# Layer-1 modulation summed along rows on VectorE, the first feature tile started by itself, and the row norm applied by a diagonal matmul

## The chip, the cores and the metric

The kernel runs on 1 core of a Trainium2 chip. Its engines are named as in the profile: PE (TensorE matmul; PEld is its weight load), DVE (VectorE), ACT (ScalarE), POOL (GpSimd) and SP (SyncE, which issues most of the DMAs). The metric is device time in microseconds (us) of one execution; lower is better. All times inside an execution count from the start of the profiled span.

## The reference

Two decoder layers on x of 512 tokens by 2048 features, in float32. Only the head of layer 1 matters here:

```python
c_act = jax.nn.silu(c)                               # c: (1, 2048)
mod = (c_act @ ada_w[0] + ada_b[0])[:, None, :]      # ada_w[0]: (2048, 6144)
shift, scale, gate = jnp.split(mod, 3, axis=-1)
h = rmsnorm(x, norm_g[0]) * (1.0 + scale) + shift    # x * rsqrt(mean(x*x) + eps) * g, then modulated
proj = h @ w_in                                      # w_in: (2048, 12288), then retention, gate, w_out
x = x + gate * y
```

The features of `h` are the contraction of `h @ w_in`, so a product with feature tile kt (128 features) can be made as soon as shift and scale of those 128 features are known. Each of the 2048 values of shift and of scale is a sum over 2048 inputs.

## The kernel before

Every product that matters is made in three float32r passes (high times high, high times low, low times high). Each operand is therefore split: ACT makes the high part with a copy to float32r (`split`, L132), DVE subtracts it from the original for the low part (L133).

**First stage (L434 to L574).** The 2048 features are 16 feature tiles, taken as 8 units of two. For each unit the stage accumulates the first head's products with three column blocks of `w_in`: "qk" (4 PSUM banks), "g" (3 banks) and "v" (4 banks), 11 outputs of 128x512, two feature tiles, three passes: 66 matmuls per unit (`products`, L403, issued at L413). PSUM has 8 banks, four in the group `acc` and four in `aux`. "g" holds three `aux` banks throughout and one is left for transposes; "qk" and "v" take turns in the four `acc` banks. When they change places, `swap` (L391) has ACT copy each bank's partial sums out to SBUF (L397) and the other's back in (L401), eight copies per change.

**Order.** `queued` (L429) pins each piece of work behind what stands last on ACT, DVE, PE and SP, so on these engines the program order is the order written. Each engine works through its own list in that order and waits at an instruction whose inputs are late.

**Modulation.** For each unit 16 tiles `aw` (`load_shift_scale`, L363) hold 2048 input rows by 256 shift and 256 scale columns, inputs on partitions (one partition has 16 of the inputs). `add_row` (L371) weights them with silu(c) and adds them up: the first on ACT (L374), the rest as 15 DVE operations of 128x512 (L376). Then PE sums over partitions with a column of ones (`sum_columns`, L385), 8 products of one column. `make_first` (L501) adds bias and norm gain (`modulate`, L245 to L249) and ACT makes h of both feature tiles twice, rounded (L268) and full (L270); DVE subtracts for the low part (L271). The rows of a unit are added up during the unit before it; the last DVE sums, PE's column sums and `make_first` stand just ahead of the products that use them.

**x and the vectors.** x arrives as eight tiles with tokens on partitions. Each token's factor rsqrt(mean square) comes from squares on ACT and DVE (`square`, L448) and a power on POOL (L128). `normalise` (L458) multiplies x by it, half on ACT (L459), half on DVE (L460). Then PE transposes each feature tile (`transpose`, L482) and ACT copies it to `xT` (L487); four tiles go ahead of the first products, two more in each unit. Ten small vectors come in by ten DMAs on POOL's queue (L229) and are turned by PE into `vcol`.

**After the stage.** DVE works out the rotary tables (`tables`, L278 to L302) after its last work on unit 7, ACT takes their sine and cosine (L304, L305), and ACT's first weight cast of the next stage (the last "g" bank of head 0, `g_r`) is queued behind them. That stage's products stand at L158 to L160.

Of the kernel before, what the change touches and what calls it, by code (L numbers as in the profile page):

```python
# [16 lines left out]
P = 128  # L17
# [32 lines left out]
def hybrid_trunk_kernel(  # L50
# [19 lines left out]
    decay,  # L70
    x_t,
    out,
):
# [27 lines left out]
    def tmp(name, shape=(P, T)):  # L101
        return base.tile(list(shape), F32, tag="tmp", bufs=6, name=name)
# [111 lines left out]

    vrows = tmp("vrows", (P, 2, P))
    DVE.memset(vrows[:, 1, :], 0.0)
    for r0, n, which, src in (
        (0, 32, 0, ada_b[0, 0 : 2 * D]),
        (32, 32, 0, ada_b[1, 0 : 2 * D]),
        (64, 16, 0, norm_g[0]),  # L220
        (80, 16, 0, norm_g[1]),
        (96, 32, 0, ret_gn_g[0]),
        (0, 4, 1, mla_q_norm_g[0]),
        (4, 4, 1, mla_kv_norm_g[0]),
        (8, 16, 1, ada_b[0, 2 * D :]),
        (24, 16, 1, ada_b[1, 2 * D :]),
        (40, 16, 1, final_norm_g),
    ):
        POOL.dma_start(vrows[r0 : r0 + n, which, :], src.rearrange("(r p) -> r p", p=P))  # L229
    vcol = base.tile([P, P + 56], F32, name="vcol")  # L230
    bias_c = (vcol[:, 0:32], vcol[:, 32:64])
    norm_c = (vcol[:, 64:80], vcol[:, 80:96])
# [9 lines left out]
    def modulate(i, ps_shift, ps_scale, k0, n):  # L242
# [3 lines left out]
        if ps_scale is not None:  # L246
# [5 lines left out]
            )  # L252

    def columns(ps, name):

        mc = small(name, 4)
        junk = tmp(f"{name}_d")
        for b in range(4):
            DVE.scalar_tensor_tensor(
                out=junk[:, b * P : (b + 1) * P], in0=ps[:, b * P : (b + 1) * P], scalar=1.0, in1=ident,  # L260
                op0=ALU.mult, op1=ALU.mult, accum_out=mc[:, b : b + 1],
            )
        return mc

# [82 lines left out]
    def first_load(kind, u):  # L347

        cn = 384 if kind == "g" else 512
        tags = (("k4b", 4), ("k4b", 4)) if kind == "g" else (("whi", 3), ("wlo", 3))  # L350
        raw = base.tile([P, 2, cn], F32, tag="raw", bufs=3, name=f"{kind}0_{u}_raw")
        c0 = {"v": 4096, "g": 8192}.get(kind)
        for dst, src in qk_parts(0, u) if kind == "qk" else [(whole, rows(w_ret_in, u, 2, c0, cn))]:
            nc.sync.dma_start(dst(raw), src)

        def prepare():
            hl = [base.tile([P, 2, cn], F32R, tag=t, bufs=n, name=f"{kind}0_{u}_{t}{i}") for i, (t, n) in enumerate(tags)]
            split(raw, *hl)
            loaded[kind, u] = hl

        return prepare

    def load_shift_scale(u, i):  # L363

        aw = l0p.tile([P, 2, 2, 256], F32, tag="aw", bufs=9, name=f"aw_{u}_{i}")
        for s in range(2):
            c0 = s * D + u * 256
            nc.sync.dma_start(aw[:, :, s, :], ada0[:, 2 * i : 2 * i + 2, c0 : c0 + 256])
        return aw

    def add_row(am, aw, k, first):  # L371
        ck = cact[:, k : k + 1]
        if first:
            ACT.activation(am, aw[:, k % 2], AF.Identity, scale=ck)  # L374
        else:
            DVE.scalar_tensor_tensor(out=am, in0=aw[:, k % 2], scalar=ck, in1=am, op0=ALU.mult, op1=ALU.add)  # L376

    def sum_columns(u, am, rest=()):

        ps = aux(f"mc_{u}")  # L380
        terms = [(aw[:, k % 2], cact[:, k : k + 1]) for k, aw in rest] + [(am, crow)]
        nt = len(terms)
        for i, (src, col) in enumerate(terms):
            for c_ in range(4):
                PE.matmul(  # L385
                    ps[:, c_ * nt + i : c_ * nt + i + 1], src[:, c_ // 2, c_ % 2 * P : (c_ % 2 + 1) * P], col,
                    start=True, stop=True,
                )
        return ps, nt

# [49 lines left out]
    first_aw = []  # L440
    for i in range(NU):
        first_aw.append(queued(load_shift_scale, 0, i))
    prepares = {("qk", 0): queued(first_load, "qk", 0)}

# [12 lines left out]

    def normalise(t):  # L458
        ACT.activation(xs[t][0], xs[t][0], AF.Identity, scale=norm[t])  # L459
# [5 lines left out]
    am = l0p.tile([P, 2, 256], F32, tag="am", bufs=2, name="am_0")  # L465
    queued(square, 0)
    queued(square, 1)
    queued(normalise, 0)
    queued(square, 2)
    queued(normalise, 1)  # L470
    queued(square, 3)
    queued(normalise, 2)
    for k in range(2):
        queued(add_row, am, first_aw[0], k, k == 0)
    queued(normalise, 3)

    xT = [k4(f"xT_{u}", F32) for u in range(NU)]

    def transpose(kt):
        ps = aux(f"xT_ps_{kt}")  # L480
        for t in range(NT):
            PE.transpose(  # L482
                ps[:, t * P : (t + 1) * P],
                xs[t][kt // 8][:, (kt % 8) // 4, (kt % 4) * P : (kt % 4 + 1) * P],
                ident,
            )
        return lambda: ACT.copy(xT[kt // 2][:, kt % 2, :], ps)  # L487

    DIRECT = 14
    for kt in range(4):  # L490
        queued(queued(transpose, kt))
    vps = aux("vps")
    queued(PE.transpose, vps[:, 0:P], vrows[:, 0, :], ident)
    queued(PE.transpose, vps[:, P : 2 * P], vrows[:, 1, :], ident)
    for k in range(2, DIRECT):
        queued(add_row, am, first_aw[k // 2], k, False)
    queued(DVE.tensor_copy, vcol, vps[:, 0 : P + 56])
    queued(prepares["qk", 0])
    mc = queued(sum_columns, 0, am, [(k, first_aw[k // 2]) for k in range(DIRECT, KD)])

    def make_first(u, mc):  # L501
        mc, nt = mc
        if nt > 1:
            sums_ = small(f"mc_{u}", 4)
            DVE.tensor_reduce(
                out=sums_, in_=mc[:, 0 : 4 * nt].rearrange("p (c i) -> p c i", i=nt), axis=AX.X, op=ALU.add
            )
            mc = sums_
        modulate(0, mc[:, 0:2], mc[:, 2:4], 2 * u, 2)
        for kt in (2 * u, 2 * u + 1):  # L510
            hT[kt] = big(f"hT_{kt}")
            yield make_h(0, kt, xT[u][:, kt % 2, :], hT[kt])

    for low in list(queued(lambda: list(make_first(0, mc)))):
        queued(low)
    swap(None, "qk")
    banks["g"] = [aux(f"g0_{b}") for b in range(3)]
    for u in range(NU):

        here, there = ("qk", "v") if u % 2 == 0 else ("v", "qk")  # L520
        more = u + 1 < NU
        aw = []
        if u > 0:
            prepares[here, u] = queued(first_load, here, u)
        prepares["g", u] = queued(first_load, "g", u)
        if more:
            aw += [queued(load_shift_scale, u + 1, i) for i in range(2)]
        prepares[there, u] = queued(first_load, there, u)
        if more:
            aw += [queued(load_shift_scale, u + 1, i) for i in range(2, NU)]  # L530
        if u > 0:
            queued(prepares[here, u])
        queued(prepares["g", u])
        if more:
            am = l0p.tile([P, 2, 256], F32, tag="am", bufs=2, name=f"am_{u + 1}")
            queued(add_row, am, aw[0], 0, True)
        lows = queued(lambda: list(make_first(u, mc))) if u > 0 else ()
        ahead = [2 * u + 4, 2 * u + 5] if 2 * u + 5 < KD else []
        if ahead:
            queued(queued(transpose, ahead[0]))  # L540
        for k in range(1, 4) if more else ():
            queued(add_row, am, aw[k // 2], k, False)
        for low in lows:
            queued(low)
        queued(prepares[there, u])
        if more:
            for k in range(4, KD):
                queued(add_row, am, aw[k // 2], k, False)
# [5 lines left out]
        if ahead:  # L554
            queued(queued(transpose, ahead[1]))
# [14 lines left out]
        queued(products, there, 2 * u)  # L570
        if more:
            mc = queued(sum_columns, u + 1, am)
        queued(products, there, 2 * u + 1)
# [1360 lines left out]
```

## Time and profile before

| | |
|---|---|
| median of 3 runs | 2227.26 us (2224.17 to 2229.06) |
| the profiled execution | 2223.61 us, its span 2221.8 us |
| PE busy, share of the span | 98% |
| DVE busy | 71% |
| ACT busy | 45% |
| first product of the first stage starts | 32.92 us |
| last product of the first stage starts | 172.62 us |
| mean granted clock of PE | 0.996 |

PE is busy nearly throughout, but its busy time is pipelined and modelled, so the stage at hand has to be read from the order of starts, not from the share. What the change touches lies in the first 190 us of the span. In a row of the timeline the first number is the start, the second the length (of a group, from its first start to its last end), and a bracket gives the engine's idle time before it and what ended it.

### The profile page before, as it was taken

Reading aid. Unit: us, or ns where it says so; the run is one execution under the profiler, and the core shown is the slowest. Engines: PE = TensorE matmul, PEld = TensorE weight load, DVE = VectorE, ACT = ScalarE, POOL = GpSimd, SP = SyncE. Lnnn points to the kernel's source line nnn. Section 1 sums busy time; section 2 is a strip of 40 time slices with the busy share of each in tenths; the row PEclk is TensorE's granted clock in tenths of the full one; section 3 lists DMA queues with packets and bytes.
Section 4 is the critical chain, followed back from the end, with each engine's and each line's share of the span. In section 5 each row is a group of like instructions: output and inputs, shape, how many; then the busy total and the mean of one; then the engine's idle time right before and its main releaser. Section 6 shows DMA issues by size and latency. Waiting matters only on the chain.

```text
span 2221.8 us, 28357 instructions
## 1 busy us (share of the span) xinstructions
PE 2170.8 (98%) x10414; PEld 1819.9 (82%) x10414; DVE 1586.6 (71%) x2397; ACT 998.5 (45%) x1496; POOL 104.2 (5%) x184
## 2 busy tenths in 40 slices
PE   5999999999999999999999999999999999999997
PEld 4887888888888888888888888898888888888886
DVE  7888867767676789656676777567977677776545
ACT  5664433434343444434344445345444355554443
POOL 1000000000001000010000000010001000000000
PEclk9999999999999999999999999999999999999998
DMA  9974586766767678573646465453458723225332
GB/s 343 353 241 168 191 282 202 261 224 218 262 198 274 220 263 296 174 239 127 232 153 226 147 211 187 137 172 108 161 185 294 251 77 95 76 96 189 123 125 90
DMA packets 238396, 437.15 MB, mean 197 GB/s; under 512 B 21032, under 2 KB 98992, under 8 KB 238256
## 3 DMA queue, kind: packets, MB, share of 16 engines
q1 hardware_dynamic: 225664, 396.16, 54.2%
q0 software_dynamic: 12160, 38.90, 4.4%
q8 instruction: 81, 1.33, 0.2%
q14 instruction: 59, 0.48, 0.1%
q10 hardware_dynamic: 432, 0.27, 0.0%
HBM read 392.27 MB, written 42.99 MB: 196 GB/s over the span
## 4 chain that ended last, share of the span: by engine, by line
PE 75%; DVE 11%; ACT 5%; issue 5%; DMA 2%; POOL 0%; SPq 0%; DVEq 0%; POOLq 0%; ACTq 0%
PE o L1161 13%; PE qk L160 4%; PE qk L158 4%; PE qk L159 4%; PE o L1861 4%; DVE am L376 2%; PE x L702 2%; PE y L703 2%; PE x L703 2%; PE y L701 2%; PE y L702 2%; PE x L701 2%; PE s L703 2%; PE s L702 2%; PE s L701 2%
## 5 line engine op out<-in xcount | busy, mean ns | idle before, releaser
L1161 PE MATMUL o<-o_h,o_whi 128*128 128x512 f32 (+1 forms) x496 | 192.5, 388 | 0.0
L1161 PE MATMUL o<-o_h,o_wlo 128*128 128x512 f32 (+1 forms) x496 | 191.6, 386 | 0.0
L1161 PE MATMUL o<-o_l,o_whi 128*128 128x512 f32 (+1 forms) x496 | 191.5, 386 | 0.0
L160 PE MATMUL qk<-hT,qk_l 128*128 128x512 f32 x448 | 175.0, 391 | 0.4 <-DVE qk_l L133 0.4
L158 PE MATMUL qk<-hT,qk_h 128*128 128x512 f32 x448 | 174.9, 390 | 0.0
L159 PE MATMUL qk<-hT,qk_h 128*128 128x512 f32 x448 | 174.5, 389 | 0.0
L864 DVE SCALAR_TENSOR_TENSOR mod_am<-mod_aw,cact,mod_am 128x1024 f32<-128x1024 f32 x120 | 153.5, 1280 | 13.5 <-DMA mod_aw<-in_ada_w_dram 12.8
L133 DVE TENSOR_TENSOR o_wlo<-o_r,o_whi 128x1024 fp32r<-128x1024 f32 x61 | 74.5, 1222 | 84.9 <-ACT o_whi L132 84.9
L133 DVE TENSOR_TENSOR qk_l<-qk_r,qk_h 128x1024 fp32r<-128x1024 f32 x56 | 68.1, 1223 | 67.7 <-ACT qk_h L132 67.3
L1161 PEld LDWEIGHTS o<-o_h,o_wlo 128*128 128x128 f32 x496 | 93.2, 188 | 18.7
L1161 PEld LDWEIGHTS o<-o_l,o_whi 128*128 128x128 f32 x496 | 93.3, 188 | 18.3
L1161 PEld LDWEIGHTS o<-o_h,o_whi 128*128 128x128 f32 x496 | 93.3, 188 | 18.1
L160 PEld LDWEIGHTS qk<-hT,qk_l 128*128 128x128 f32 x448 | 84.1, 188 | 19.4 <-DVE qk_l L133 2.1
L159 PEld LDWEIGHTS qk<-hT,qk_h 128*128 128x128 f32 x448 | 84.1, 188 | 17.3
L158 PEld LDWEIGHTS qk<-hT,qk_h 128*128 128x128 f32 x448 | 84.2, 188 | 17.2
L132 ACT CAST qk_h<-qk_r 128x1024 fp32r<-128x1024 f32 x56 | 57.8, 1049 | 88.7 <-PE qk L159 73.5
L376 DVE SCALAR_TENSOR_TENSOR am<-aw,cact,am 128x512 f32<-128x512 f32 x118 | 88.7, 751 | 3.6
L158 PE MATMUL g<-h,g_h 128*128 128x512 f32 x232 | 90.7, 391 | 0.3 <-ACT g_h L132 0.3
L159 PE MATMUL g<-h,g_h 128*128 128x512 f32 x232 | 90.4, 389 | 0.0
L160 PE MATMUL g<-h,g_l 128*128 128x512 f32 x232 | 89.9, 390 | 0.0
L132 ACT CAST o_whi<-o_r 128x1024 fp32r<-128x1024 f32 x61 | 63.5, 1052 | 21.9 <-issue 10.1
L133 DVE TENSOR_TENSOR o_w_lo<-o_w_raw,o_w_hi 128x1024 fp32r<-128x1024 f32 x32 | 38.9, 1220 | 34.6 <-ACT o_w_hi L132 34.5
(1256 smaller groups left out, 5996.0 us busy)
## 6 DMA issues: line engine op xcount, KB each, us to landing
mod_aw<-in_ada_w_dram SPq DMA_DIRECT2D x128, 512.0 KB, 5.3
aw<-in_ada_w_dram SPq DMA_DIRECT2D x128, 256.0 KB, 6.0
o_r<-in_ret_w_out_dram SPq DMA_DIRECT2D x64, 512.0 KB, 4.4
qk_r<-in_ret_w_in_dram SPq DMA_DIRECT2D x112, 256.0 KB, 3.8
g_r<-in_mla_w_in_dram SPq DMA_DIRECT2D x32, 512.0 KB, 4.3
o_w_raw<-in_mla_w_out_dram SPq DMA_DIRECT2D x32, 512.0 KB, 3.8
qk_d<-qk_st POOLq DMA_DIRECT2D x32, 256.0 KB, 3.7
qk_r<-qk_d SPq DMA_DIRECT2D x32, 256.0 KB, 6.3
```

Of the source, the lines that this page charges most:

```text
L132: ACT.copy(hi, src)
L133: DVE.tensor_sub(lo, src, hi.bitcast(F32))
L158: PE.matmul(o, lhs[0], rhs[0], start=first and not seeded, stop=False, skip_group_check=seeded)
L159: PE.matmul(o, lhs[0], rhs[1], start=False, stop=False, skip_group_check=seeded)
L160: return PE.matmul(o, lhs[1], rhs[0], start=False, stop=last, skip_group_check=seeded)
L376: DVE.scalar_tensor_tensor(out=am, in0=aw[:, k % 2], scalar=ck, in1=am, op0=ALU.mult, op1=ALU.add)
L701: PE.matmul(banks[b], a[0], w[0], start=first, stop=False, skip_group_check=True)
L702: PE.matmul(banks[b], a[0], w[1], start=False, stop=False, skip_group_check=True)
L703: PE.matmul(banks[b], a[1], w[0], start=False, stop=True, skip_group_check=True)
L864: DVE.scalar_tensor_tensor(out=am, in0=aw, scalar=ck, in1=am, op0=ALU.mult, op1=ALU.add)
L1161: PE.matmul(o, w[i][:, ki, c0 + b * P : c0 + (b + 1) * P], a[j], start=first and i + j == 0, stop=last and i == 1, skip_group_check=True,)
L1861: PE.matmul(banks2[b][:, cols], w[0][i][:, 0, b * P : (b + 1) * P], o2_moving(w, u, cols)[j], start=u + i + j == 0, stop=u == KD - 1 and i ...
```

## The change

- The weights of shift and scale come from a transposed copy of `ada_w[0]` made with the inputs, outputs on partitions: one tile `aw` of 128 outputs by 2048 inputs for each feature tile and each of shift and scale, four buffers of it instead of nine of the old. One DVE operation multiplies it by silu(c) and sums along the row (`sum_mod`); nothing is left for PE. Feature tile 0 is loaded and summed in two halves.
- For that silu(c) must stand on every partition: c is loaded to one partition, PE spreads it with four float32 products of 128x512 with ones, and ACT takes their silu (`c_all`), ahead of the squares.
- `make_first` works on one feature tile. The stage starts with tile 0 alone, "v" first: v(0), g(0), a swap, qk(0), qk(1), g(1), a swap, v(1).
- In each unit u the preparation of unit u+1 is now written ahead of the products of u (`prepare_ahead`: the casts of all three weight tiles and h of the first feature tile), and the second tile's h behind the swap (`prepare_behind`).
- The token factor is no longer multiplied into x: DVE makes a diagonal of it, and the transposes become matmuls with that diagonal. Six tiles go ahead of the first products.
- The ten small vectors are laid out with the inputs and come by one DMA.

What each engine gets in one unit, in program order (unit u's products, unit k = u+1 prepared; "here" and "there" are "qk" and "v", which change places from unit to unit):

```
SP    here(k), aw(2k,shift), aw(2k,scale), g(k), aw(2k+1,shift), there(k), aw(2k+1,scale)
DVE   sum(2k,shift), low of here(k), sum(2k,scale), a and b of 2k, sum(2k+1,shift), low h(2k),
      low of g(k), sum(2k+1,scale), a and b of 2k+1, low of there(k), low h(2k+1)
ACT   high of here(k), h(2k) twice, high of g(k), high of there(k), xT copy, 8 swap copies, h(2k+1) twice, xT copy
PE    here(2u), here(2u+1), diagonal matmuls, g(2u), g(2u+1), there(2u), diagonal matmuls, there(2u+1)
```

The diff, cut to its core:

```diff
-    def load_shift_scale(u, i):
-        aw = l0p.tile([P, 2, 2, 256], F32, tag="aw", bufs=9, name=f"aw_{u}_{i}")
...
+    def load_mod(kt, s):
+        aw = l0p.tile([P, D], F32, tag="aw", bufs=4, name=f"aw_{kt}_{s}")
+        n = 2 if kt == 0 else 1
+        for j in range(n):
+            cols = slice(j * D // n, (j + 1) * D // n)
+            nc.sync.dma_start(aw[:, cols], ada_t[s * D + kt * P : s * D + (kt + 1) * P, cols])
         return aw
-    def add_row(am, aw, k, first):
-    def sum_columns(u, am, rest=()):
...
+    def sum_mod(kt, s):
+        aw, n = mods[kt, s], 2 if kt == 0 else 1
+        col = small(f"mc_{kt}_{s}", n)
+        for j in range(n):
+            cols = slice(j * D // n, (j + 1) * D // n)
+            DVE.scalar_tensor_tensor(
+                out=aw[:, cols], in0=aw[:, cols], scalar=1.0, in1=c_all[:, cols], op0=ALU.mult, op1=ALU.mult,
+                accum_out=col[:, j : j + 1],
+            )
...
+    c_all = l0p.tile([P, D], F32, name="c_all")
+    ACT.dma_start(c_all[0:1, :], c)
+    for j in range(4):
+        cols = slice(j * T, (j + 1) * T)
+        ps = aux(f"c_ps{j}")
+        PE.matmul(ps, ones[0:1, :], c_all[0:1, cols], start=True, stop=True)
+        ACT.activation(c_all[:, cols], ps, AF.Silu)
...
-    def normalise(t):
-        ACT.activation(xs[t][0], xs[t][0], AF.Identity, scale=norm[t])
-        DVE.tensor_scalar(out=xs[t][1], in0=xs[t][1], scalar1=norm[t], scalar2=None, op0=ALU.mult)
+    def diagonal(t):
+        diags.append(l0p.tile([P, P], F32, tag="diag", bufs=4, name=f"x_diag{t}"))
+        DVE.tensor_scalar(out=diags[t], in0=ident, scalar1=norm[t], scalar2=None, op0=ALU.mult)
...
-            PE.transpose(
+            PE.matmul(
                 ps[:, t * P : (t + 1) * P],
                 xs[t][kt // 8][:, (kt % 8) // 4, (kt % 4) * P : (kt % 4 + 1) * P],
-                ident,
+                diags[t], start=True, stop=True,
             )
...
+    def prepare_ahead(u, first=None):
+        here, there = ("qk", "v") if u % 2 == 0 else ("v", "qk")
+        low = queued(prepares[here, u])
+        queued(sum_mod, 2 * u, 0)
+        if first is not None:
+            queued(first)
+        queued(low)
+        queued(sum_mod, 2 * u, 1)
+        low = queued(make_first, 2 * u)
+        queued(sum_mod, 2 * u + 1, 0)
+        queued(low)
+        low = queued(prepares["g", u])
+        late[u] = queued(prepares[there, u])
+        queued(low)
+        queued(sum_mod, 2 * u + 1, 1)
+
+    def prepare_behind(u):
+        low = queued(make_first, 2 * u + 1)
+        queued(late[u])
+        queued(low)
+
+    load_unit(1)
+    queued(queued(prepares["v", 0]))
+    for s in range(2):
+        queued(sum_mod, 0, s)
+    low = queued(make_first, 0)
+    queued(sum_mod, 1, 0)
+    queued(low)
+    lows = [queued(prepares[kind, 0]) for kind in ("g", "qk")]
+    for low in lows:
+        queued(low)
+    queued(sum_mod, 1, 1)
+    swap(None, "v")
+    queued(products, "v", 0)
...
+    queued(products, "g", 0)
+    queued(swap, "v", "qk")
+    low = queued(make_first, 1)
+    queued(products, "qk", 0)
+    prepare_ahead(1, low)
...
         if more:
             queued(swap, here, there)
+            prepare_behind(u + 1)
```

More of the change, by code (lines that the diff above doesn't have):

```diff
@@ L213, in hybrid_trunk_kernel @@
     ACT.activation(cact, cact, AF.Silu)
[L215 to L229, printed above, removed]
     vcol = base.tile([P, P + 56], F32, name="vcol")
+    POOL.dma_start(vcol, vecs)
     bias_c = (vcol[:, 0:32], vcol[:, 32:64])
@@ L252, in modulate @@
             )
[L254 to L263, printed above, removed]
     def make_h(i, kt, src, dst):
@@ L391, in swap, with make_first @@
+    def make_first(kt):
+        k1 = slice(kt, kt + 1)
+        DVE.tensor_add(b_col[0][:, k1], mods[kt, 0], bias_c[0][:, k1])
+        DVE.scalar_tensor_tensor(
+            out=a_col[0][:, k1], in0=mods[kt, 1], scalar=bias1[:, k1], in1=norm_c[0][:, k1], op0=ALU.add, op1=ALU.mult
+        )
+        hT[kt] = big(f"hT_{kt}")
+        return make_h(0, kt, xT[kt // 2][:, kt % 2, :], hT[kt])
     def swap(old, new):
@@ L494, in hybrid_trunk_kernel @@
[L494 to L512, printed above, removed]
@@ L514, in hybrid_trunk_kernel, with load_unit @@
-    for low in list(queued(lambda: list(make_first(0, mc)))):
-        queued(low)
-    swap(None, "qk")
-    banks["g"] = [aux(f"g0_{b}") for b in range(3)]
-    for u in range(NU):
+    def load_unit(u):
+        here, there = ("qk", "v") if u % 2 == 0 else ("v", "qk")
+        load_first(here, u)
+        load_mods(2 * u)
+        load_first("g", u)
+        mods[2 * u + 1, 0] = queued(load_mod, 2 * u + 1, 0)
+        load_first(there, u)
+        mods[2 * u + 1, 1] = queued(load_mod, 2 * u + 1, 1)
@@ L520, in hybrid_trunk_kernel @@
+    queued(products, "g", 0)
[3 more added lines that the diff above has]
+    prepare_ahead(1, low)
+    queued(products, "qk", 1)
+    queued(queued(transpose, 6))
+    queued(products, "g", 1)
+    queued(swap, "qk", "v")
+    prepare_behind(1)
+    queued(queued(transpose, 7))
+    queued(products, "v", 1)
+    for u in range(1, NU):
         here, there = ("qk", "v") if u % 2 == 0 else ("v", "qk")
         more = u + 1 < NU
-        aw = []
-        if u > 0:
-            prepares[here, u] = queued(first_load, here, u)
@@ L525, in hybrid_trunk_kernel @@
-        prepares["g", u] = queued(first_load, "g", u)
+        ahead = [2 * u + 6, 2 * u + 7] if 2 * u + 7 < KD else []
         if more:
[L527 to L548, printed above, removed]
+            load_unit(u + 1)
@@ L570, in hybrid_trunk_kernel @@
         queued(products, there, 2 * u)
-        if more:
-            mc = queued(sum_columns, u + 1, am)
+        for kt in ahead[1:]:
+            queued(queued(transpose, kt))
         queued(products, there, 2 * u + 1)
```

78 lines of the change are left out of this document (42 added, 36 removed).

## The prediction

> **What bounds the stage now.** I read the windows first (start:end, length, then busy time of PE, PEld, DVE, ACT and POOL, the granted clock, DMA share, GB/s), then the timelines of DVE, PE and ACT for one unit, then those of the start and of the end.
>
> ```profile
> span 2221.8 us, 28357 instructions
> 8.00:14.00 6.00, 0.95 (x2) 0.37 (x2) 4.04 (x10) 5.18 (x7) 2.29 (x4) 1.00 1.03 408
> 48.00:50.00 2.00, 0.76 (x7) 0.49 (x5) 1.97 (x3) 0.45 (x1) 0.00 (x0) 1.00 1.10 347
> 52.00:54.00 2.00, 2.00 (x6) 1.52 (x5) 1.93 (x4) 2.00 (x4) 0.00 (x0) 0.50 1.10 348
> 60.00:100.00 40.00, 39.95 (x193) 32.65 (x192) 36.85 (x53) 27.87 (x44) 0.00 (x0) 1.00 1.09 353
> L376 DVE SCALAR_TENSOR_TENSOR am<-aw,cact,am 128x512 f32<-128x512 f32 x118 | 88.7, 751 | 3.6
> 85.17 1.22 DVE L133 TENSOR_TENSOR v_wlo<-v_raw,v_whi 128x1024 fp32r<-128x1024 f32 x1
> 86.31 0.95 DVE L133 TENSOR_TENSOR g_k4b<-g_raw,g_k4b 128x768 fp32r<-128x768 f32 x1
> ...
> 102.48 1.22 DVE L133 TENSOR_TENSOR qk_wlo<-qk_raw,qk_whi 128x1024 fp32r<-128x1024 f32 x1
> 85.53 0.95 PE L385 MATMUL mc<-ones,am 128*128 128x1 f32 x8
> ...
> 95.10 0.60 PE L482 MATMUL xT_ps<-ident,x 128*128 128x128 f32 x4
> 95.45 4.38 PE L413 MATMUL g<-hT,g_k4b 128*128 128x512 f32 x18
> 99.67 0.39 PE L413 MATMUL qk<-hT,qk_whi 128*128 128x512 f32 x1
> ...
> 100.57 0.39 PE L413 MATMUL qk<-hT,qk_whi 128*128 128x512 f32 x1
> ```
>
> A unit takes 17.3 us (low of "here" to low of "here", 85.17 to 102.48). Of that PE's products need 15.0: 18 of "g" in 4.22 (95.45 to 99.67) and 48 at 0.225 (99.67 to 100.57 is four); two transposes add 0.35 each, so 15.7, which no rearrangement here can beat. The column sums (85.53) take 0.95, which makes 16.7 and leaves 0.6 for all of PE's waits. DVE needs 15 adds x 0.751 = 11.3, two lows of 1.14 (85.17 to 86.31), one of 0.95 and smaller ones: it is busy 92% from 60 to 100, close behind PE. DMA runs at 353 GB/s there. So with the column sums gone and nothing else in PE's way a unit could gain 1.6.
>
> **The start.** Columns: start, length, idle before and its releaser.
>
> ```profile
> 14.63 1.22 DVE L450 SCALAR_TENSOR_TENSOR x_sq<-x 128x1024 f32<-128x1024 f32 x1 [0.26 <-DMA x<-in_x_dram]
> 15.78 0.08 DVE L450 DVE_READ_ACCUMULATOR x_sq<-x 128x1 f32 x1
> 17.41 1.15 ACT L459 ACTIVATE x<-x,x_r 128x1024 f32<-128x1024 f32 x1 [0.50 <-POOL x_r L128]
> 19.13 0.58 ACT L487 COPY xT<-xT_ps 128x512 f32<-128x512 f32 x1 [0.56 <-PE xT_ps L482]
> 19.98 0.58 ACT L487 COPY xT<-xT_ps 128x512 f32<-128x512 f32 x1 [0.27 <-PE xT_ps L482]
> 32.92 0.80 PE L413 MATMUL qk<-hT,qk_whi 128*128 128x512 f32 x1 [0.67 <-ACT hT L268]
> 33.51 0.63 PE L413 MATMUL qk<-hT,qk_wlo 128*128 128x512 f32 x1
> 33.94 0.63 PE L413 MATMUL qk<-hT,qk_whi 128*128 128x512 f32 x1
> 1487.48 0.68 PE L906 MATMUL x_r<-x_diag,ones 128*128 128x128 f32 x4
> ```
>
> Gone ahead of the first product are 14 adds, PE's column sums, the vectors' transposes and 1.15 on ACT plus the DVE half of `normalise`. The last token factor is there at 17.41, its diagonal about 17.65. Ahead of the squares ACT now also waits for PE to spread c: four cold products, 0.43 each at the cold rate of 33.51 to 33.94, and four silus; some of that lies beside the wait for x, so I put the last diagonal at 18.0 (17.65 to 18.4). The page "FP8 and Floating Point Precision" of the Trainium skill (Matmul Precision, TensorE Precision Notes) says that true float32 takes four passes through PE; by that the four would cost 1.72 each. The four float32 products of 128x128 at 1487.48 took 0.68 together, at most 0.17 each, which does not look like four passes; the rule stays as a rival below.
>
> From 18.0 on: six transposed tiles go through ACT 0.85 apart (19.13 to 19.98), and only then comes the high of v(0) (1.05), its low on DVE (1.14), and only behind that the four half sums. A sum over 1024 takes 1.15 and a read of 0.08 (14.63, 15.78): 1.23, with the two adds and `make_first` about 5.65 in all. Sum: 18.0 + 0.5 + 6 x 0.85 + 1.05 + 1.14 + 5.65 puts the first h at 31.1 to 31.4, and with one ACT operation (0.82) the first product at 32.0 instead of 32.92. So the start gains 1 us, not the ten that the removed adds suggest: `aw` is there, but the sums are queued behind v's low and that behind six copies.
>
> **The loop in each unit.** The rows that carry it:
>
> ```profile
> 78.55 0.59 ACT L487 COPY xT<-xT_ps 128x512 f32<-128x512 f32 x1 [3.88 <-PE xT_ps L482]
> 79.04 0.59 ACT L397 COPY part_qk<-qk 128x512 f32<-128x512 f32 x1
> ...
> 83.91 1.05 ACT L132 CAST v_whi<-v_raw 128x1024 fp32r<-128x1024 f32 x1
> 84.86 0.84 ACT L132 CAST g_k4b<-g_raw 128x768 fp32r<-128x768 f32 x1
> 85.60 0.72 ACT L374 ACTIVATE am<-aw,cact 128x512 f32<-128x512 f32 x1
> 87.62 0.82 ACT L268 ACTIVATE hT<-xT,b_col,a_col 128x512 fp32r<-128x512 f32 x1 [1.30 <-DVE a_col L249]
> 88.35 0.80 ACT L270 ACTIVATE h_6f<-xT,b_col,a_col 128x512 f32<-128x512 f32 x1
> 33.60 0.69 DVE L271 TENSOR_TENSOR hT<-h_0f,hT 128x512 fp32r<-128x512 f32 x1 [1.65 <-ACT h_0f L270]
> ```
>
> A sum over 2048 isn't in this trace. From the row of 1024: 1.15, 1.06 for 1024 elements more (DVE's lows go from 0.69 at 512 to 1.22 at 1024, 0.53 per 512) and 0.08 of read, 2.3. Bounds: 2.0 (the adds' 0.751 at 512 against 1.15 at 1024, 0.4 per 512) and 3.0 (four times 0.751); I take 2.30, whose row has the same form with a sum along the row. DVE's work falls from about 17.0 to 9.2 + 2 x 1.14 + 0.9 + 2 x 0.69 + 0.6 = 14.4 per unit, below PE's 15.7. DVE is no longer the bound by its sum; but the program order closes a loop over three engines. With S the first copy of a swap in unit u:
> - swap, eight copies on ACT, 4.87 (79.04 to 83.91); then h of the second tile, 0.73 and 0.80 (87.62, 88.35): S+6.4;
> - DVE's low of that h, 0.65: S+7.05; only behind it the sum of the next unit's first shift, 2.30: S+9.35;
> - the high of the next "here" takes one of three weight buffers, whose last reader is "there" just swapped in: after the eighth copy 3 products, the transposes and 12 products (3.8), S+8.95, and 1.05 on ACT: S+10.0; its low on DVE, 1.14: S+11.2;
> - the sum of scale, 2.30: S+13.5; b and a, 0.15 each as an estimate (the read's 0.08 and a gap): S+13.8;
> - h of the next first tile twice, high of "g", high of "there", one copy to `xT`, in ACT's order and start to start 0.73 + 0.7 + 0.74 + 0.95 + 0.49 (78.55 to 79.04) = 3.6: S+17.4. Only there stands the next swap.
>
> So a unit takes 17.4, with PE waiting some 1.7 of it at the four banks that the swap fills 1.24 apart. The last units without transposes come to 16.9 and 16.5, the first to 16.7: S(0) to S(6) is 16.7 + 3 x 17.4 + 16.9 + 16.5 = 102.3, plus 0.1 for the hand-overs of each of six periods: 102.9. From the first h (31.1) to S(0) goes another chain of DVE and ACT: the four long sums 9.2, the lows of h, "g" and "qk" 2.7, b and a, a second h, and 3.6 on ACT: 17.7, S(0) = 48.8. S(6) = 151.7. From there 4.98 for the swap, 15 products (3.4) and the last unit's 66 (14.95): the last product ends at **175.0**.
>
> New transfers: one row of 8 KB per partition and tile instead of pieces of 1 KB. Bytes per unit stay 5.6 MB, 16.0 us at the 353 GB/s of the window, 13.8 at the 408 of the x loads: either is hidden in 17.4. The ten small loads become one; nothing waits for them. The diagonal products cost 0.35 to 0.68 a tile (rows 95.10 and 1487.48), I take 0.4; PE's slack of 1.7 hides it, and without that slack it would cost 0.1 to 0.7 per unit.
>
> **The end of the stage.**
>
> ```profile
> 161.87 0.43 DVE L282 CAST ret_sin<-ret_pi 128x512 f32<-128x512 int32 x1 [0.38 <-DMA ret_pi<-in_positions_dram]
> 171.94 1.07 PE L413 MATMUL qk<-hT,qk_whi 128*128 128x512 f32 x4
> 172.31 0.63 ACT L304 ACTIVATE ret_sin<-ret_sin 128x512 f32<-128x512 f32 x1 [5.36 <-DVE ret_cos L302]
> 174.53 0.50 PE L158 MATMUL g<-hT,g_h 128*128 128x512 f32 x1 [1.53 <-ACT g_h L132]
> 187.01 0.39 PE L158 MATMUL qk<-hT,qk_h 128*128 128x512 f32 x1
> ```
>
> Before, the last product ends at 172.85 and the following "qk" starts at 187.01: 48 products (10.9) and 3.3 of waits, because the tables hold DVE from 161.87 to 172.3 and `g_r`'s cast stands behind their sine on ACT. After, unit 7 has no sums, so DVE is through with its low of h at S(6) + 7 = 158.7 and with the tables at 169.3, nearly 6 ahead of the last product. I count 2.5 of the 3.3 as gone: 175.0 + 10.9 + 0.8 = 186.7, 0.3 earlier than before. Span 2221.5; with the 1.8 around it (2223.61 less 2221.8) 2223.3. The median of the runs lies 3.65 above the profiled execution, so I forecast **2227.0**, no change. (0.2%, 4.45 us, is about what a measurement of this kernel can tell from none.)
>
> **Rivals.**
> - *A, the loop doesn't close, PE bounds (chance 0.12).* If the long sum is at its lower bound (two on the loop, 0.6 less) and the cast of "here" isn't held (0.7 less), the loop falls to 16.1, beside PE's 15.8: six periods of 1.3 and 1.1 at the start (four sums), 9 less: 2218. For it: DVE's sum of work is 14.4. Against: the order above is written out, and its terms are rows.
> - *B, slower: the clock falls at the bank waits (0.16).* In before, PE had 0.76 busy in 48 to 50, and at 52 to 54 the clock was 0.50 with products at 0.43: 12 of them cost 2.4. In the new kernel every unit has four waits in a row, and the 15 products behind them release the cast of "here": a dip there lengthens the loop itself. In three to seven units: 7 to 17, 2234 to 2244, middle 2238. It decides as soon as PE is idle long enough in one stretch; in before 1.24 idle out of 2 was enough, 0.6 has no row. The page "TensorE: Matmul & The Clock Gate" of the Trainium skill (What's actually happening) throttles after an idle window of about 3.4 us, by which waits of 0.6 would never do it; but by that rule the dip at 52 would not have come either.
> - *C, c's four products at four times the 0.43 (0.06).* The last diagonal is then 3.5 later (three times 0.43 more for each of four products, less what waits anyway), all else follows: 2230.5.
> - *D, loop longer by hops or by late `aw` (0.09).* Each of the loop's nine hand-overs 0.1 more, six periods: 5, 2232. A sum of 3.0 would give 1.4 per period, 8, 2235.
>
> **How the numbers follow.** The loop as worked out has 0.57, its own range 2222 to 2232 from the sum's bounds (start 1.5 either way, 0.3 per period downwards and, for a sum of 2.5, 0.4 upwards); of that 0.05 is faster, 0.09 slower. With A, faster is 0.17; with B and D, slower is 0.34; with C, same is 0.49. The range 2220 to 2238 leaves out A and half of B, 0.20.
>
> **What would show it.** First product at 32.0, with the six copies and v's low ahead of the sums; sums of 2048 at 2.2 to 2.3; swaps 17.4 apart in the middle units; PE's waits at the swap's copies (1 to 2 per unit); no DVE wait on `aw` beyond the start; last product's end at 175.0; the wait on `g_h` at the next stage gone. Swaps 15.8 apart would be A; granted clock 0.50 in 2-us windows behind the swaps, B; first copy to `xT` after 22, C.

## The result, and the profile after

The changed kernel takes 2230.88 us (median of 12 runs, 2229.36 to 2232.51), the kernel before 2224.73 in the same comparison (12 runs): ratio 1.0024, 95% interval 1.0016 to 1.0033. It is slower by about 6 us, where no change was forecast; the time itself lies inside the stated range. The profiled execution took 2229.62, near the lower end of these runs; its span was 2227.8, 6.0 more than before.

The start first. ACT, then PE and DVE (start, length, what ended the idle time before):

```profile
8.07 0.60 ACT L450 ACTIVATE c_all<-c_ps 128x512 f32<-128x512 f32 x1 [3.00 <-PE c_ps L449]
...
13.19 0.60 ACT L450 ACTIVATE c_all<-c_ps 128x512 f32<-128x512 f32 x1 [1.11 <-PE c_ps L449]
13.68 1.05 ACT L458 ACTIVATE x_sq<-x 128x1024 f32<-128x1024 f32 x1
...
22.35 0.59 ACT L496 COPY xT<-xT_ps 128x512 f32<-128x512 f32 x1 [4.41 <-PE xT_ps L491]
24.05 0.59 ACT L496 COPY xT<-xT_ps 128x512 f32<-128x512 f32 x1 [1.12 <-PE xT_ps L491]
...
29.66 1.05 ACT L335 CAST v_whi<-v_raw 128x1024 fp32r<-128x1024 f32 x1
37.29 0.81 ACT L245 ACTIVATE hT<-xT,b_col,a_col 128x512 fp32r<-128x512 f32 x1 [6.58 <-DVE a_col L372]
```

```profile
5.99 7.16 PE L449 MATMUL c_ps<-c_all,ones 1*128 1x512 f32 x8 [5.99 <-DMA c_all<-in_c_dram]
...
20.79 8.36 PE L491 MATMUL xT_ps<-x_diag,x 128*128 128x128 f32 x44 [1.06 <-DVE x_diag L471]
38.16 0.79 PE L400 MATMUL v<-v_whi,hT 128*128 128x512 f32 x1 [9.01 <-ACT hT L245]
```

```profile
21.17 0.29 DVE L471 TENSOR_SCALAR x_diag<-ident,x_r 128x128 f32<-128x128 f32 x1 [0.44 <-POOL x_r L130]
30.74 1.23 DVE L337 TENSOR_TENSOR v_wlo<-v_raw,v_whi 128x1024 fp32r<-128x1024 f32 x1 [9.28 <-ACT v_whi L335]
31.89 1.22 DVE L358 SCALAR_TENSOR_TENSOR aw<-aw,c_all 128x1024 f32<-128x1024 f32 x1
```

The program has four products for c; the trace has eight instructions (x8), and the four silus come 1.71 apart (8.07, 9.78, 11.48, 13.19). ACT works in order and can't begin the squares before 13.68, so the last diagonal is ready at 21.46. Then come the six sets of diagonal products (a set is the four products of one feature tile), by their copies 1.70 apart at first and 0.89 for the last two. The first product starts at 38.16 instead of 32.92. DVE's sums start at 31.89, behind v's low, for which DVE stood idle 9.28 until ACT had made v's high. The data had long been there: `start` below begins the same sums at 22.56 without a wait for a transfer.

The loop, by the first copy of each swap on ACT, then one unit:

```profile
54.56 0.58 ACT L384 COPY part_qk<-qk 128x512 f32<-128x512 f32 x1
...
71.10 0.58 ACT L384 COPY part_v<-v 128x512 f32<-128x512 f32 x1
...
89.10 0.58 ACT L384 COPY part_qk<-qk 128x512 f32<-128x512 f32 x1
...
159.31 0.57 ACT L384 COPY part_qk<-qk 128x512 f32<-128x512 f32 x1
```

```profile
80.71 1.06 ACT L335 CAST v_whi<-v_raw 128x1024 fp32r<-128x1024 f32 x1 [2.16 <-PE qk L400]
85.53 0.82 ACT L245 ACTIVATE hT<-xT,b_col,a_col 128x512 fp32r<-128x512 f32 x1 [3.76 <-DVE a_col L372]
```

```profile
76.87 1.05 PE L491 MATMUL xT_ps<-x_diag,x 128*128 128x128 f32 x8
77.68 0.47 PE L400 MATMUL qk<-hT,qk_whi 128*128 128x512 f32 x1
```

The distances are 16.54, then three of 18.0 (to 107.12 and 125.13), 17.5 and 16.65 (142.66, 159.31). The loop closes as forecast: ACT stands idle for PE ahead of the cast, and for DVE's `a_col` ahead of h. Its middle units are 0.5 longer than forecast. The set between the swapped-in products takes 0.81 (76.87 to 77.68).

The end, on PE: the first "g" and the first "qk" of the next stage.

```profile
182.79 0.39 PE L160 MATMUL g<-hT,g_h 128*128 128x512 f32 x1
...
193.67 0.39 PE L160 MATMUL qk<-hT,qk_h 128*128 128x512 f32 x1
```

10.88 from one to the other: the 48 products without a wait. The next stage's "qk" starts 6.66 later than before (187.01); that is the loss.

### The profile page after: what moved, and what is told of

The parts are those of the page before. It is cut to its first block, busy times and chain, and to the rows that moved or that the text cites. A ratio compares the mean times of both kernels' runs of the same rounds, so it can differ in the third digit from the quotient of the medians.

```text
span 2227.8 us, 28061 instructions
## 1 busy us (share of the span) xinstructions
PE 2176.3 (98%) x10404; PEld 1818.1 (82%) x10404; DVE 1569.4 (70%) x2355; ACT 995.7 (45%) x1496; POOL 100.5 (5%) x175
## 4 chain that ended last, share of the span: by engine, by line
PE 78%; DVE 9%; ACT 7%; issue 5%; DMA 1%; POOL 0%; ACTq 0%; POOLq 0%; DVEq 0%
PE o L1181 13%; PE qk L162 4%; PE qk L160 4%; PE qk L161 4%; PE o L1881 4%; PE x L722 2%; PE x L723 2%; PE y L723 2%; PE y L721 2%; PE y L722 2%; PE x L721 2%; PE s L723 2%; PE s L722 2%; PE s L721 2%; PE g L160 2%
## 5 line engine op out<-in xcount | busy, mean ns | idle before, releaser
L161 PEld LDWEIGHTS qk<-hT,qk_h 128*128 128x128 f32 x448 | 84.1, 188 | 17.3
L358 DVE SCALAR_TENSOR_TENSOR aw<-aw,c_all 128x2048 f32<-128x2048 f32 (+1 forms) x34 | 73.3, 2159 | 0.0
```

Source lines behind the costliest of these rows:

```text
L161: PE.matmul(o, lhs[0], rhs[1], start=False, stop=False, skip_group_check=seeded)
L358: DVE.scalar_tensor_tensor(out=aw[:, cols], in0=aw[:, cols], scalar=1.0, in1=c_all[:, cols], op0=ALU.mult, op1=ALU.mult, accum_out=col[:, ...
```

## The experiments

Every time below is the median in its own comparison; the kernel before has 2225 there unless said. "End" is the start of the next stage's first "g" product (182.79 in the changed kernel).

**c spread with its silus late** (`spread_late`).

```diff
-        ACT.activation(c_all[:, cols], ps, AF.Silu)
...
     queued(square, 3)
+    for j in range(4):
+        queued(spread_silu, j)
     queued(diagonal, 2)
```

> Theory (true float32 products cost four passes, and what stands behind them on ACT moves with them): with c's four silus queued behind the squares on ACT, the squares run as x arrives, the last diagonal is ready at about 18 instead of 21.5, the first product starts at about 34.7 instead of 38.2, every swap keeps its distance (16.5, 18.0, 18.0 ...), and the run is 3.4 us shorter than the changed kernel, about 2227.4. Rival (the start waits for the rows of aw or of v to land, the spread is hidden): the first product stays within 0.5 of 38.2 and the time within 1 us of 2230.9.

Measured 2226.42, ratio 1.0004 (0.9995 to 1.0013) to before. ACT and PE:

```profile
18.13 0.59 ACT L501 COPY xT<-xT_ps 128x512 f32<-128x512 f32 x1 [1.66 <-PE xT_ps L496]
19.84 0.59 ACT L501 COPY xT<-xT_ps 128x512 f32<-128x512 f32 x1 [1.12 <-PE xT_ps L496]
20.74 0.59 ACT L501 COPY xT<-xT_ps 128x512 f32<-128x512 f32 x1 [0.32 <-PE xT_ps L496]
...
23.91 1.05 ACT L335 CAST v_whi<-v_raw 128x1024 fp32r<-128x1024 f32 x1
```

```profile
32.39 0.79 PE L400 MATMUL v<-v_whi,hT 128*128 128x512 f32 x1 [9.01 <-ACT hT L245]
```

The first copy comes 4.2 earlier, the first product 5.8 (3.5 expected). The surplus of 1.6 behind the first copy is the sets' pace: their copies come 0.9 apart from the second on, where the changed kernel had 1.70 for the first four. End at 176.99, 5.8 earlier. The start was not waiting for `aw` or v.

**c rounded before the spread** (`spread_fp32r`, one execution).

```diff
-        PE.matmul(ps, ones[0:1, :], c_all[0:1, cols], start=True, stop=True)
+        PE.matmul(ps, c_ones, c_r[j // 2][0:1, j % 2, :], start=True, stop=True)   # both float32r
```

> The changed kernel with c rounded to float32r before PE spreads it (the rounding of c is what it leaves out); order unchanged. Theory (a true float32 product of 512 columns is two instructions of two passes, 1.71 cold): one instruction of 0.43 each, the four silus 0.4 to 0.6 apart instead of 1.71, the squares start at about 9 to 10 instead of 13.7, the first product at 32 to 35. Rival (the spread is slow because its operand has one row and the clock is low, whatever the type): silus 1.1 or more apart, squares at 12 or later.

```profile
7.67 2.06 ACT L455 ACTIVATE c_all<-c_ps 128x512 f32<-128x512 f32 x4 [2.60 <-PE c_ps L454]
9.60 1.08 ACT L463 ACTIVATE x_sq<-x 128x1024 f32<-128x1024 f32 x1
```

2225.31 in this execution. All four silus stand back to back in 2.06, the squares start at 9.60, the first product at 32.60, and the end is 177.17: both 5.6 earlier, against 5.8 with the order changed. The order, the shapes and the one-row operand are those of the changed kernel; this kernel leaves out what the rounding takes from c. So it is the type of the product that costs.

**The factor multiplied into x again** (`no_diag`): `diagonal` replaced by the `normalise` of before, the products by transposes with `ident`.

> Only the norm's factor is put back into x (ACT and DVE multiply, PE transposes with the identity). Theory (a diagonal product is two instructions of two passes each): the six sets ahead of the first product go 0.85 apart instead of 1.7, less 1.15 for the multiplication on ACT, first product 1.3 to 1.7 earlier (36.5 to 36.9); a set in the loop takes 0.35 instead of 0.81, which brings the cast of the next weights 0.45 forward and the middle swaps from 18.0 to 17.55 apart, five times; together 3.4 to 4 us shorter, about 2227. Rival (the sets lie under ACT's copies and PE's slack): start 1.2 later for the multiplication, swaps stay 18.0 apart, 1 us longer than the changed kernel.

Measured 2231.15, 1.0024 (1.0015 to 1.0033) to before: no gain over the changed kernel, against the expectation. The stage did what was expected but for the start: middle swaps 17.55 apart (one 18.03), first product only 0.5 earlier, because the multiplications stand between the squares on ACT; end at 180.92, 1.9 earlier. In the profiled execution that was lost again far behind. Windows of this kernel, then the same of the changed kernel (granted clock third from the end):

```profile
1416.00:1418.00 2.00, 2.00 (x6) 1.52 (x6) 0.56 (x2) 0.00 (x0) 0.00 (x0) 0.51 0.73 244
...
1790.00:1792.00 2.00, 2.00 (x8) 2.00 (x8) 1.99 (x7) 0.30 (x1) 0.00 (x0) 0.50 0.63 173
```

```profile
1416.00:1418.00 2.00, 2.00 (x10) 1.68 (x9) 1.82 (x7) 0.00 (x0) 0.00 (x0) 1.00 0.34 72
...
1790.00:1792.00 2.00, 2.00 (x11) 1.78 (x10) 1.88 (x6) 0.32 (x3) 0.00 (x0) 1.00 0.74 193
```

The clock falls at two places of unchanged code where the changed kernel's profiled execution keeps it. This kernel is 1.3 ahead at the last "y" product before the first place, 0.3 behind after it (DVE's first reading of `x_r`, 1494.8 against 1494.5) and 1.8 behind after the second (the first product with `pt`, 1807.15 against 1805.34). Each kernel has one trace, so it is not shown that the other executions lost it at the same places. In its one execution with a mean granted clock of 0.996 `no_diag` took 2228.47; the changed kernel's two with 0.995 took 2229.36 and 2229.62. So the gain of 1.9 at the stage's end can be read from the stage's own marks, but not from the median.

**Order of the sums in the units** (`loop`).

```diff
+    high = low
     low = queued(make_first, 2 * u)
+    if high is not None:
+        queued(high)
...
 def prepare_behind(u):
     low = queued(make_first, 2 * u + 1)
     queued(late[u])
+    if u + 1 < NU:
+        load_unit(u + 1)
+        for s in range(2):
+            queued(sum_mod, 2 * u + 2, s)
     queued(low)
...
         if more:
-            load_unit(u + 1)
             prepare_ahead(u + 1)
```

> Only the order in the units changes: DVE makes both sums of the next unit's first tile before the low of the second tile's h and before the low of the next weights. Theory (the loop over swap, h, low, sum, low, sum, h, swap sets the unit): the loop is cut, PE with 15.0 of products and two sets of 0.81 sets the unit, middle swaps 16.7 to 16.9 apart instead of 18.0, last product's end 5 to 7 earlier (176 to 178 instead of 182.8), about 2225. Rival (the swap's eight copies with PE waiting at each bank set the unit): swaps stay within 0.3 of 18.0 and the time within 2 us of 2230.9.

```profile
66.17 0.59 ACT L384 COPY part_v<-v 128x512 f32<-128x512 f32 x1
...
82.94 0.59 ACT L384 COPY part_qk<-qk 128x512 f32<-128x512 f32 x1
```

Middle swaps are 16.77 apart instead of 18.0 (the next at 99.71), as expected. The first distance is 12.85 instead of 16.54, which was not expected, and the end is 171.38, 11.4 earlier instead of 5 to 7. Of that 1.2 arose at the start, where the same program's sets were faster in this execution. 2222.46, 0.9984 (0.9975 to 0.9993). The loop of the prediction is shown: cutting DVE's part of it, with no work removed, takes PE's waits at the swap away (none from 66 to 132, where the changed kernel had 3.1 from 71 to 143). The edit also issues each unit's loads earlier; that is not what helped, as DVE waits for no `aw` in the changed kernel's units, and in `loop` it does, for 6.0 in all.

**Order of the start** (`start`).

```diff
+    v0_low = queued(prepares["v", 0])
-    for kt in range(6):
+    for kt in range(2):
         queued(queued(transpose, kt))
+    first_copies = [queued(transpose, kt) for kt in range(2, 6)]
...
     low = queued(make_first, 0)
+    for copy in first_copies:
+        queued(copy)
```

> Only the start's order changes: the cast of v ahead of the copies to xT, two copies instead of six ahead of the first h; the spread and the diagonals stay. Theory (the long sums stand behind v's low and that behind six copies, not behind data): the sums start at about 22.7 instead of 31.9, the first product at about 28.7 instead of 38.2, the first swap of qk to v at about 46 instead of 54.6; unit distances as in the changed kernel; 8 to 9 us shorter, about 2222. Rival (aw lands late): the sums start where aw lands, DVE shows idle time ended by a DMA, and less than 4 us is won.

```profile
28.83 0.50 PE L400 MATMUL v<-v_whi,hT 128*128 128x512 f32 x1 [0.80 <-ACT hT L245]
```

First product at 28.83, 9.3 earlier, with the same spread and the same diagonals; first swap at 46.90, 7.7 earlier; end 175.06. 2223.47, 0.9990 (0.9982 to 0.9999). The sums start at 22.56 instead of 31.89 and wait for no transfer, so the rival is out. Reordering this queue brings the end forward by 7.7; taking the spread off the path brought 5.8.

**Both prices off the path** (`both`: the edits of `spread_late` and `no_diag`).

> The changed kernel with the spread's silus behind the squares and the norm's factor multiplied into x as before. Both mis-sized products are then off the path, so if nothing else was wrong this kernel should follow the prediction's own sum: first product 32.0 to 32.4, first swap of qk to v 48.8, middle swaps 17.5 apart, last product's end 175.0, next stage's qk at 186 to 187 and about 2224 to 2227, no different from the kernel before by more than 2 us. Rival (other terms were wrong too and cancel): any of these marks off by more than 1.

```profile
11.66 1.15 ACT L471 ACTIVATE x<-x,x_r 128x1024 f32<-128x1024 f32 x1 [2.20 <-POOL x_r L130]
12.72 1.04 ACT L461 ACTIVATE x_sq<-x 128x1024 f32<-128x1024 f32 x1
```

2226.15, 1.0006 (0.9997 to 1.0015): no change from before, as the prediction's sum had it. Its marks: first product 33.56, first swap 49.96, middle swaps 17.55, end 176.64, the next stage's "qk" 187.83. The middle distances fit; the other marks are 0.8 to 1.6 late. Of that 1.2 enters at the start, where ACT's third square comes at 12.72 behind a multiplication instead of 10.82 as in `spread_late`, and 0.3 in one unit of 17.84, in which the granted clock fell to 0.50 (70 to 72). So the rival's condition is met in part; what enters at the start comes from the normalising, which this kernel has and the changed one does not.

**The diagonal alone in the kernel before** (`before_diag`).

> The kernel before with nothing changed but the norm's factor as a diagonal and the transposes as products with it. Theory (a set of four true float32 products costs 0.81 on PE, 0.46 more than four transposes, and PE has only 0.6 of waits in a unit of 17.3): the start stays where the adds put it (first product within 0.7 of 32.9), units of two sets become 17.7 to 18.2, six of them, 3 to 5.5 longer, 2228 to 2231. Rival (DVE's adds set the unit and hide it): units stay within 0.2 of 17.3 and the time within 1.5 of before.

```profile
49.75 1.02 PE L385 MATMUL mc<-ones,am 128*128 128x1 f32 x8 [1.84 <-DVE am L376]
```

2227.79, 1.0016 (1.0007 to 1.0024), just under the expected 2228 to 2231. First product 33.13; by DVE's lows the four middle units are 18.0 to 18.1 instead of 17.3, as expected; the next stage's first "g" comes at 176.90 against 174.53, 2.4 later. Four times 0.75 is 3.0. The first unit gave 0.7 back (17.85 against 18.55): the dip of the clock at 52, which is in before, is missing here (1.00 from 50 to 56), although PE stood idle longer ahead of it, 1.84 against 1.24. DVE did not hide the sets.

**Versions that beat both** (`all`: all four edits; `all_diag`: without `no_diag`; `mix`: diagonals for tiles 0 to 7, POOL multiplies the second half of x, identity transposes from tile 8; `mix2`: the same with POOL's multiplications behind its four factors).

```diff
+    for t in range(NT):
+        with behind(mybir.EngineType.Pool, V_):        # this line in mix2 only
+            POOL.tensor_scalar(out=xs[t][1], in0=xs[t][1], scalar1=norm[t], scalar2=None, op0=ALU.mult)
```

> Four edits together: silus behind the squares, factor multiplied into x, the start's order (cast of v first, two copies ahead of h), the order of the sums in the units. Theory (start and loop were both matters of order, and add up): first product at about 25.5, middle swaps 15.7 to 15.9 apart, set by PE, last product's end at 154 to 157, 16 to 22 us less than the kernel before, 2203 to 2209. Rival (transfers bound: 5.6 MB per unit at 353 GB/s is 16.0): swaps 16 or more apart with DVE's sums ended by DMA, 2209 or more.

> As the one with all four edits, but with the diagonal matrices kept. Theory (a set costs 0.81 on PE instead of 0.35, two in each unit, PE sets the unit): first product at about 25, middle swaps 16.7 to 16.8 apart, 4 to 6 us longer than with the factor multiplied into x. Rival (the diagonal pays at the start by what ACT saves): within 1 us of it.

> The silus late, the start's order, the sums' order, the diagonals for feature tiles 0 to 7 only; POOL multiplies the factor into the second half of x meanwhile, and tiles 8 to 15 are transposed with the identity. Theory (the diagonal pays at the start, where it takes 3.5 off the first product, and costs 0.7 per unit later, where PE sets the unit): first product at 25, middle swaps from tile 8 on 16.1 apart instead of 16.8, last product's end 2 to 3 before that of the version with diagonals throughout (159 to 160), 2207 to 2209. Rival (POOL's four multiplications slow DVE or come late): the swaps from 43 to 75 grow by over 1, nothing is won.

> As the mixed version, but POOL's four multiplications of the second half of x stand behind its four token factors instead of between them. Theory (in the mixed version the last factor came 5 late because POOL's 4-us multiplications stood ahead of it, nothing else): the last diagonal is ready at 18 again, first product at 25 instead of 31.6, swaps from tile 8 on 16.1 apart, the next stage's first product at 159 to 160 instead of 165.7, 2207 to 2210. Rival (POOL's multiplications slow DVE's sums while they run, 18 to 34): DVE's half sums take over 1.4 each and the first product starts after 26.

| | median | ratio to before (interval) | first product | middle swaps | end |
|---|---|---|---|---|---|
| `all` | 2211.74 | 0.9941 (0.9927 to 0.9955) | 28.39 | 16.07 | 162.47 |
| `all_diag` | 2210.82 | 0.9938 (0.9924 to 0.9952) | 24.93 | 16.77 | 161.82 |
| `mix` | 2214.18 | 0.9955 (0.9941 to 0.9969) | 31.63 | 16.07 | 165.72 |
| `mix2` | 2208.95 (before 2226.84) | 0.9925 (0.9912 to 0.9939) | 26.95 | 16.06 | 160.31 |

Start and loop add up: against the changed kernel `spread_late`, `start` and `loop` gain 4.5, 7.4 and 8.4, together 20.3, and `all_diag`, which has all three, gains 20.1. `all` came out 2.7 above its upper bound: its first product was 2.9 late, with the cast of v behind the multiplications on ACT. As worded, its rival is met: 16.07 looks like the transfers' 16.0, the time is over 2209, and DVE does wait for `aw` (the window, then DVE's waits from 60 to 140):

```profile
60.00:124.00 64.00, 64.00 (x294) 52.12 (x293) 56.22 (x70) 45.48 (x69) 0.00 (x0) 1.00 0.94 356
DVE aw L358 <- DMA aw<-in_ada_t_dram: 6.6, 10, 2.0
```

But PE is busy in all 64 us of the window and no product of it waits for a transfer, so 16.07 is set at PE, and the 15.7 of the prediction was 0.35 short. Of this 0.18 stands behind the transpositions: after each of the two the second product starts 0.31 behind the first instead of 0.23. Most of the rest stands at the banks that are being swapped, where PE's weight loads wait for ACT four times in the window, 0.3 each. With diagonals the swaps are 16.77 apart. `all_diag` gives that back by its earlier start, so the rival had it there: 0.65 earlier at the end, not 4 to 6 later. The 0.9 between the two medians lies within the overlap of their intervals.

`mix` failed for the reason that its POOL rows show: from the second on each factor stands behind a multiplication, and the last is there at 23.15. Beside them stand DVE's wait for it (from 20 on) and a half sum that took 2.06 instead of 1.22 while POOL multiplied, so the rival (POOL slows DVE or comes late) was right at the start. The swaps from 43 to 75 did not grow.

```profile
15.05 3.99 POOL L513 TENSOR_SCALAR x<-x,x_r 128x1024 f32<-128x1024 f32 x1
19.02 0.56 POOL L130 TENSOR_TENSOR x_r<-x_v,mhalf 128x1 f32<-128x1 f32 x1
...
22.59 0.56 POOL L130 TENSOR_TENSOR x_r<-x_v,mhalf 128x1 f32<-128x1 f32 x1
DVE x_diag L474 <- POOL x_r L130: 3.3, 1, 3.3
24.52 2.06 DVE L358 SCALAR_TENSOR_TENSOR aw<-aw,c_all 128x1024 f32<-128x1024 f32 x1
```

With the order pinned, `mix2` has the lowest ratio, 0.75% below the kernel before. Its end is 1.5 earlier than that of `all_diag`, but the intervals of the two ratios overlap. Its first product came at 26.95, not at the expected 25, and 2.0 later than that of `all_diag`; the last section comes back to that.

## Why the prediction was wrong

The sum against the trace, term by term:

| term | forecast | measured | off |
|---|---|---|---|
| last diagonal | 18.0 | 21.46 | +3.5 |
| six copies, until v's high | 5.6 | 8.2 | +2.6 |
| v's high to first h | 7.8 | 7.6 | -0.2 |
| first h to first swap | 17.7 | 17.3 | -0.4 |
| six units | 102.9 | 104.75 | +1.85 |
| last swap to last product's end | 23.3 | 23.5 | +0.2 |
| to the next stage's qk | 11.7 | 10.9 | -0.8 |

(The first h was forecast at 31.1 to 31.4; the chain went on from 31.1.)

**The step that failed is one price, the true float32 product, on which three terms rest.** The prediction took 0.43 for each of c's products and 0.4 for a set of diagonal products in the loop, and it left the six sets of the start at the 0.85 of the old transposes. The runs showed 1.71 for each of c's products, 0.81 for a set in the loop and 1.70 for a set at the start. The low price came from the row at 1487.48 (x4, 0.68), which was read as four products. The kernel makes two there (its `spread` is called for two): the row counts instructions, and each float32 product is two of them. So the trace of before held the right price (0.34 at most for each product, not 0.17), and the changed kernel's x8 for four products says the same.

The page "FP8 and Floating Point Precision" of the Trainium skill (Matmul Precision, TensorE Precision Notes) has true float32 at four passes. The runs agree: 512 columns take 1.71 where a float32r product takes 0.43, and a warm set, which has 512 columns in all, takes 0.81 where a warm float32r product takes 0.225 (3.6 times). Four transposes take 0.35. The prediction weighed that rule and dismissed it by the misread row. Rival C, with a chance of 0.06, had its 3.5 at the last diagonal right, but left the diagonals out.

- *The start.* The queue was read rightly: `spread_late` and `spread_fp32r` move the first product by what the spread costs and by the sets' pace behind it. `start` moves it 9.3 by order; 6.7 of that is the forecast length of the queue (six copies and v's high), the rest the sets. The queue's size was wrong by the price and by PE's pace: four of the six sets went 1.70 apart, the last two 0.89. Transposes at the start stay 0.85 apart, as forecast (`no_diag`). In `loop`, whose start is the same program, the faster pace came earlier, and the +2.6 of the table was +1.4.
- *The loop* closed link by link, and `loop` shows it by cutting it. Its middle units were forecast 0.5 too short: the set on the path to the cast of "here" takes 0.81 where the sum had 0.4, and with transposes in its place the swaps are 17.55 apart (`no_diag`), against 17.5 forecast. The sentence that PE's slack hides the set is refuted, because the set stands ahead of the products that release the weight buffer, on the loop itself; the prediction's own 3.8 for that path contains it. Rival A did not come; PE waited at the banks.
- *Rival B.* The changed kernel's trace has no dip between the first swap of "qk" to "v" and the end of the stage. In `no_diag` two came behind swaps, at 56 to 60 and 72 to 78; the second one's unit was 18.03 instead of 17.55. So the mechanism exists, at 0.5 and not at 2.4. The 2.4 was too high from the start: seven products at 52 ran at 0.43, not 12, which with a slowed transposition makes 1.6. The condition was wrong as well. Idle time in one stretch does not decide: `before_diag` had 1.84 and no dip, before had 1.24 and a dip. What does is open.
- *The end* was right: the wait for `g_h` is gone, and with it the 0.8 of waits that the sum had kept.
- *The median.* The three runs of before at hand had 2227.26; twelve have 2224.73. That hid part of the error in the time, not in the ratio: the next stage's "qk" came 7.0 later than forecast (193.67 against 186.7), the time is only 3.9 above 2227.0. It is luck that rival C's 2230.5 lies so near the measured 2230.88; its "qk" would have been at 190.2.

The table's differences lead from the forecast to the measured 193.67 by construction; the test of the account is `both`. With both products off the path, its "qk" starts at 187.83, so 5.8 of the 7.0 are gone, and the time does not differ from before.

## What to carry to other kernels

Before pricing an operation from a row, count the operations in the program: a row's x can be twice the number of products, as here, and dividing by it then gives half the price. PE's spare time did not hide the added operation here, because the release of a buffer stood behind it. Walk the loop from one buffer's release to the next, over all engines, and put the new operation into it. Where a sum of work has fallen below the bound and the time has not, look for order: two short reorderings (`start` 7.4, `loop` 8.4) were each worth more than the 6 that the whole change cost.

## What the runs showed of the hardware

- The half speed of PE at the start is not in the granted clock's column. In the changed kernel the sets from 22 to 27 ran at 1.70 each, the next two at 0.89 and later ones at 0.81, and the column says 1.00 throughout:

```profile
22.00:30.00 8.00, 7.14 (x42) 6.95 (x41) 0.00 (x0) 3.75 (x7) 0.00 (x0) 1.00 0.72 279
```

- Beside POOL's long multiplications some DVE operations took 0.4 to 0.9 longer, about one for each multiplication, and the others kept their time. In `mix2` these were three short ones (the add of one column takes 0.16 in the changed kernel, the diagonal 0.29), while the half sums between them stayed at 1.22, and the operations for b and a at 25.66 and 25.77 at 0.15 and 0.22. `mix2`, POOL, then DVE:

```profile
16.95 14.48 POOL L514 TENSOR_SCALAR x<-x,x_r 128x1024 f32<-128x1024 f32 x4
```

```profile
16.99 1.15 DVE L474 TENSOR_SCALAR x_diag<-ident,x_r 128x128 f32<-128x128 f32 x1 [0.47 <-POOL x_r L130]
...
21.59 0.87 DVE L364 TENSOR_TENSOR mc_0b<-mc 128x1 f32<-128x1 f32 x1
24.78 0.95 DVE L364 TENSOR_TENSOR mc_1b<-mc 128x1 f32<-128x1 f32 x1
```

The two adds (0.7 and 0.8 more) and what the diagonal moved v's low (0.5) are the 2.0 by which `mix2` starts later than `all_diag`. Short length is not the reason: in `mix` a half sum took 2.06 (24.52, above) and a square on DVE 1.66 instead of 1.22, while the diagonals and the adds of its half sums kept 0.29 and 0.16. What picks the operation that waits was not tried.
